# Experts of a mixture, two at a time in plain float32 in the two halves of the array's columns

## The chip, the cores and the metric

The program runs on one core of one Trainium2 chip, as one launch. The metric is device microseconds of the whole program, from its first to its last instruction and what the launch adds around them. Times of single instructions come from one profiled execution on that core, in microseconds from the start of its span.

## What is computed

Two transformer blocks run one after the other on 256 tokens of width 1024, all in float32. The first block (two layers: attention with a gated MLP, a pooling mixer, and after each a product-key expert layer) and the mixer of the second block are not touched by the change. The change is in the last layer, a hierarchical mixture of experts, which every token enters with two of 32 experts:

```python
def hier_moe(v, w_grp, b_grp, w_exp, b_exp, w_gate, w_up, w_down):
    ...
    w = p_grp * p_in / jnp.sum(p_in, axis=-1, keepdims=True)
    expert_id = g_sel * MOE_EXPERTS_PER_GROUP + e_sel
    combine = jnp.einsum('tk,tke->te', w, jax.nn.one_hot(expert_id, MOE_N_EXPERTS, dtype=f32))
    y = jnp.zeros(vt.shape, f32)
    for e in range(MOE_N_EXPERTS):
        hdn = jax.nn.silu(vt @ w_gate[e]) * (vt @ w_up[e])
        y = y + (combine[:, e:e + 1].astype(hdn.dtype) * hdn) @ w_down[e]
    return y.reshape(bsz, seq, d).astype(v.dtype)
```

Per expert w_gate and w_up are 1024 x 512 and w_down is 512 x 1024. All 32 experts' weights are read once: 192 units of 128 x 2048 floats (1 MiB each), six per expert: two for the gate, two for up, two for down.

## The kernel before

The last layer is `moe` (line 1405). It first makes the mixer's last product (`wout2`), the norm and the routing; `rk` then holds each token's place among its expert's tokens, up to CAP = 64 places per expert (a branch at the end, line 1710, serves experts with more; the trace shows none of it). The loop over the 32 experts follows (the `for n in range(32)` in `moe`). For one expert it does this:

- **Weights.** Each 1 MiB unit is loaded by SP's queue (`raw`, L161) into one of seven buffers (three of `raw_p`, four named `more`, carved from a large tile that the profile calls `room`). `halves` and `split` (L149, L150) then turn each half unit into a high part, by ScalarE, and the rest as a low part, by VectorE. Both are float32r, the type that TensorE takes in one pass. Five pairs of buffers hold the parts.
- **Tokens.** `place` and `gather` (L1542, L1550, L1553) make, for four experts at once, one-hot matrices and with them the gathered tokens `xg`, high and low parts side by side as 2 x 64 columns.
- **Gate and up.** `hidden` calls `lin2` (L1595, L1596): stationary are the 128 columns of an expert's tokens (64 high, 64 low), moving the weights' high part and then the low part, 512 columns each. That is 32 products for gate and up.
- **Merge and transpose.** The high and the low rows are added and turned by products with `pair` (L1618), Silu and the product of gate and up follow (L1621, L1622), and a split of the result into `hT`.
- **Down.** 16 more products in `lin2`, then the places' rows times their weights: `y` (L1634, L1635, or L1639 for one half of the columns, kept in plain float32).
- **Scatter.** Products with the one-hot `GT` add `y` to four accumulators in PSUM (L1645). `back` (L1582 to L1584) makes `GT` and the weights of the places.

The order on each engine is set when the program is built: the calls above are recorded, the small ones (`jobs`) placed by a rate between the products of `lin2`, and a scheduler then moves instructions where dependences allow. Each engine, and SP's queue of loads, then runs its list in order; a load waits until its buffer's last reader is done.

Of the kernel before, what the change touches and what calls it, by code (L numbers as in the profile page):

```python
# [9 lines left out]
F32 = mybir.dt.float32  # L10
F32R = mybir.dt.float32r
# [19 lines left out]
class Carve:  # L31
    """tiles of one stage, all float32 or integer, in [lo, hi) KB of larger tiles"""
# [37 lines left out]
def weave(main, other, rate):  # L70
    """main with rate steps of other after each of its own"""
    owed = 0.0
    for _ in main:
        owed += rate
        while owed >= 1:
            next(other, None)
            owed -= 1


def both(a, b):  # L80
    """steps of a and b in turn"""
# [11 lines left out]
def early(it, n):  # L93
    """the same, but n items ahead are made"""
    q = []
    for v in it:
        q.append(v)
        if len(q) > n:
            yield q.pop(0)
    yield from q  # L100


class Net:
    def __init__(self, es, tc, A):
# [5 lines left out]
        self.hl_p = ep(tc.tile_pool(name="hl_p", bufs=3))  # L110
        self.rings()
        self.nhl, self.more_hl = 0, []
# [20 lines left out]
    def room(self, es, *kbs):  # L133
        """large float32 tiles"""
# [18 lines left out]
    def rings(self, more=(), first=()):  # L153
        """where the loads go in turn: first, and then more and the three of raw_p over and over"""
# [9 lines left out]
    def halves(self, ap):  # L164
        r = self.raw(ap)
        w = ap.shape[-1] // 2
        for j in range(2):
            k = self.nhl % (3 + len(self.more_hl))
            self.nhl += 1
            hi, lo = self.more_hl[k - 3] if k > 2 else (self.hl_p.tile([P, 1024], F32R, tag=t, name=self.nm(t))  # L170
                                                        for t in ("hi", "lo"))
# [12 lines left out]
    def lin_steps(self, units, N, K, targets):  # L184
        """targets: (psum [128, N], fn(k) -> (hi, lo) stationary [128, 128]); a step for every k"""
# [13 lines left out]
    def squares(self, x, tt, h, parts):  # L199
        """parts[:, 2 * tt + h] = sum of squares of half a row, over the row's 1024"""  # L200
# [3 lines left out]
    def rstd(self, x=None, parts=None):  # L204
        """[128, 2] of (mean square of x's rows + eps) ** -0.5"""
# [29 lines left out]
    def trans_split(self, src, hh, hl, nk, scale=None, bias=None, full=None):  # L235
        """src [128, 2, nk*128] -> hh, hl [128, nk, 256], optionally scaled and shifted per row of the result"""
# [28 lines left out]
    def bcast(self, dst, cols):  # L265
        """dst [128, 1024]: every row holds the 1024 values of cols [128, 8]"""
# [20 lines left out]
    def mod_pair(self, l, order, pool, works):  # L287
        """chunks of 512 values, for the sequence and for the context; works run in between"""
# [24 lines left out]
    def mod_rows(self, l, n0, n1, pool):  # L313
        """chunks for the sequence alone, by the tensor engine; a step for every half unit"""
# [21 lines left out]
    def mod_chunks(self, l, n0, n1, cb):  # L336
        """the same by the vector engine, cb: the condition in every row; a step for every unit"""
# [13 lines left out]
    def mod_scale(self, g_cols, sc_cols):  # L351
        """g * (1 + sc) as [128, 8]"""
# [4 lines left out]
    def resid(self, x, accs, gb, pool, then=None):  # L357
        """x += gb * accs;  accs[tt][half] psum"""
# [10 lines left out]
    def resid_rstd(self, x, accs, gb, pool):  # L369
        """the same, and the new rows' inverse root mean squares"""  # L370
# [5 lines left out]
    def mixer0(self, x, pool):  # L376
# [53 lines left out]
        # keys twice, for the two halves of the partitions  # L430
# [5 lines left out]
        def axial(dst, src, tt, nh):  # L436
            """dst [128, nh, 64] = rope(src)"""
# [16 lines left out]
        # [(head of the pair, d), pair, t]  # L454
# [25 lines left out]
        # attention, a pair of heads at a time  # L480
# [53 lines left out]
        # gMLP  # L534
# [51 lines left out]
    def peer_pre(self, l, x, r, hh, hl, pool):  # L586
        """the modulated second norm, transposed and split; r: the inverse root mean squares of x"""
# [6 lines left out]
    def peer(self, l, after):  # L594
        """-> accs[tt][half], psum tiles of the [256, 1024] result"""
# [7 lines left out]
        def rows(i, n):  # L603
            """S[:, i:i + n], within one half"""
# [7 lines left out]
        # the routing's working space lies where the last products come  # L612
# [11 lines left out]
        # of the sums of two sorted sixteens the best sixteen have (a + 1) * (b + 1) <= 16:  # L624
        # rows of 16, 8, 4 and 2 columns hold them, in the order of a * 16 + b
# [35 lines left out]
        def routing():  # L661
# [10 lines left out]
            for tt in range(2):  # L672
# [14 lines left out]
                # column c of the candidates: row a and column b  # L687
# [1293 lines left out]
```

## Time and profile before

| | |
|---|---|
| time, median of 3 runs | 2728.44 us (2725.46 to 2731.94) |
| span of the profiled execution | 2725.8 us |
| TensorE busy over the span | 2633.1 us (97%) |
| VectorE busy | 2128.4 us (78%) |
| ScalarE busy | 1728.3 us (63%) |
| read from memory | 592.49 MB, 219 GB/s over the span |

The profile gives the span of the execution (first to last instruction) and no other time of its own; the median of the runs is 2.6 us above it. In the last quarter of the span, from about 2106 us on, lies the layer that is changed: of forty equal slices of the span, the last nine show transfers at some 340 GB/s, TensorE busy at 90% or more and both other engines at 80 to 90%, until the last slice.

### The profile page before, as it was taken

What the parts mean: (1) busy time and instruction counts of PE and PEld (TensorE: products, weight loads), DVE (VectorE), ACT (ScalarE), POOL (GpSimd) and SP (SyncE); (2) the same over time, 40 slices, a digit from 0 to 9 for tenths busy, and PEclk for the clock granted to TensorE, in tenths of its full rate; (3) what the DMA queues carried; (4) which work ended last, traced back from release to release, by engine and by line L of the source; (5) the groups of instructions that cost most, each with busy time, mean ns of one, the idle gap of its engine ahead of it and who ended that gap; (6) DMA issues with size and microseconds to landing.
All of it is one profiled execution on the core that took longest, in us unless ns stands there. A gap on an engine that the chain in (4) does not pass through costs nothing. (4 is left out here: it accounts for less than half of the span.)

```text
span 2725.8 us, 42575 instructions
## 1 busy us (share of the span) xinstructions
PE 2633.1 (97%) x16114; PEld 2250.3 (83%) x16114; DVE 2128.4 (78%) x3881; ACT 1728.3 (63%) x3024; POOL 24.8 (1%) x28
## 2 busy tenths in 40 slices
PE   8989999999999999999999999998999899999997
PEld 4679999999888879999999888886777777677775
DVE  3666998897589864998898656667767898888887
ACT  4454547886444544454887544455665798888886
POOL 0000000000000000000000000000000000000000
PEclk9999999999999999999999999999999899999999
DMA  6454554335589833455333655554426799899994
GB/s 262 185 187 170 195 188 176 127 139 197 219 337 365 336 119 141 171 195 193 140 140 140 223 186 185 196 184 146 156 93 217 272 363 340 339 340 348 338 347 186
DMA packets 86818, 598.47 MB, mean 220 GB/s; under 512 B 10430, under 2 KB 12366, under 8 KB 15694
## 3 DMA queue, kind: packets, MB, share of 16 engines
q1 hardware_dynamic: 80608, 583.73, 58.0%
q10 hardware_dynamic: 5998, 11.94, 1.3%
q8 instruction: 129, 2.11, 0.3%
q14 instruction: 83, 0.68, 0.1%
HBM read 592.49 MB, written 3.15 MB: 219 GB/s over the span
## 5 line engine op out<-in xcount | busy, mean ns | idle before, releaser
L150 DVE TENSOR_TENSOR lo<-raw,hi 128x1024 fp32r<-128x1024 f32 x744 | 897.4, 1218 | 283.6 <-ACT hi L149 281.7
L149 ACT CAST hi<-raw 128x1024 fp32r<-128x1024 f32 x744 | 770.6, 1050 | 428.2 <-PE mm L740 247.4
L739 PE MATMUL mm<-hh,hi 128*128 128x256 f32 x2048 | 577.4, 282 | 0.0
L741 PE MATMUL mm<-hh,lo 128*128 128x256 f32 x2048 | 568.3, 278 | 0.3 <-DVE lo L150 0.3
L740 PE MATMUL mm<-hl,hi 128*128 128x256 f32 x2048 | 567.8, 277 | 0.0
L177 PE MATMUL acc<-hi,hh 128*128 128x512 f32 (+1 forms) x1312 | 512.4, 394 | 2.1 <-ACT hh L149 1.6
L179 PE MATMUL acc<-hi,hl 128*128 128x512 f32 (+1 forms) x1312 | 514.2, 392 | 0.0
L178 PE MATMUL acc<-lo,hh 128*128 128x512 f32 (+1 forms) x1312 | 513.5, 391 | 0.1
L740 PEld LDWEIGHTS mm<-hl,hi 128*128 128x128 f32 x2048 | 386.2, 189 | 0.0
L741 PEld LDWEIGHTS mm<-hh,lo 128*128 128x128 f32 x2048 | 384.9, 188 | 0.8 <-DVE lo L150 0.5
L739 PEld LDWEIGHTS mm<-hh,hi 128*128 128x128 f32 x2048 | 385.0, 188 | 0.0
L150 DVE TENSOR_TENSOR lo<-room,hi 128x1024 fp32r<-128x1024 f32 x270 | 319.6, 1220 | 49.3 <-ACT hi L149 48.2
L149 ACT CAST hh<-room 128x256 fp32r<-128x256 f32 x272 | 109.3, 406 | 316.8 <-PE acc L178 306.8
L177 PEld LDWEIGHTS acc<-hi,hh 128*128 128x128 f32 x1312 | 247.0, 188 | 56.4 <-issue 2.2
L178 PEld LDWEIGHTS acc<-lo,hh 128*128 128x128 f32 x1312 | 247.4, 189 | 52.0 <-DVE lo L150 0.9
L179 PEld LDWEIGHTS acc<-hi,hl 128*128 128x128 f32 x1312 | 247.2, 188 | 51.4
L149 ACT CAST hi<-room 128x1024 fp32r<-128x1024 f32 x270 | 273.0, 1057 | 14.6 <-PE acc L179 12.9
L1596 PE MATMUL mm<-lo,xg 128*128 128x512 f32 x512 | 230.8, 451 | 19.1 <-DVE lo L150 19.1
L1595 PE MATMUL mm<-hi,xg 128*128 128x512 f32 x512 | 202.3, 396 | 0.0
L150 DVE TENSOR_TENSOR hl<-room,hh 128x256 fp32r<-128x256 f32 x272 | 111.7, 422 | 92.5 <-ACT hh L149 92.2
L1596 PEld LDWEIGHTS mm<-lo,xg 128*128 128x128 f32 x512 | 96.2, 188 | 72.5 <-DVE lo L150 45.1
L791 PE MATMUL mm<-room 128*128 128x128 f32 x1024 | 132.3, 275 | 0.4 <-ACT room L785 0.4
(469 smaller groups left out, 3512.9 us busy)
## 6 DMA issues: line engine op xcount, KB each, us to landing
raw<-in_dn SPq DMA_DIRECT2D x128, 1024.0 KB, 4.8
room<-in_moe SPq DMA_DIRECT2D x109, 1024.0 KB, 5.6
raw<-in_up SPq DMA_DIRECT2D x103, 1024.0 KB, 4.8
raw<-in_moe SPq DMA_DIRECT2D x83, 1024.0 KB, 5.4
room<-in_up SPq DMA_DIRECT2D x25, 1024.0 KB, 6.7
raw<-in_modt SPq DMA_DIRECT2D x24, 1024.0 KB, 6.1
raw<-in_w2in SPq DMA_DIRECT2D x18, 1024.0 KB, 4.8
raw<-in_wq SPq DMA_DIRECT2D x16, 1024.0 KB, 4.8
```

The source lines that it names most:

```text
L149: self.nc.scalar.copy(hi, src)
L150: self.last_lo = self.nc.vector.tensor_tensor(lo, src, hi.bitcast(F32), ALU.subtract).ins
L177: mm(ps, xh, wh, start=start, stop=False)
L178: mm(ps, xh, wl, start=False, stop=False)
L179: mm(ps, xl, wh, start=False, stop=stop)
L739: mm(o, wh, hh[:, k, :], start=(k == 0), stop=False)
L740: mm(o, wh, hl[:, k, :], start=False, stop=False)
L741: mm(o, wl, hh[:, k, :], start=False, stop=(k == KD - 1))
L791: mm(ps[:, j * P:(j + 1) * P], B[:, j, :], Am[:, j, :], start=True, stop=True)
L1595: mm(ps, get(k + j), hi[:, w], start=(k + j == 0), stop=False)
L1596: mm(ps, get(k + j), lo[:, w], start=False, stop=(k + j == K - 1))
```

## The change

Experts go through the loop in pairs, 16 turns instead of 32. The weights are no longer split: TensorE reads the loaded units as plain float32, in which each product is two passes (two instructions). The tokens of a pair are gathered as plain float32 too (high and low parts are summed in PSUM by the gather). One expert's 64 places are stationary in columns 0 to 63 of the array and write partitions 0 to 63 of a PSUM tile, the other's in columns 64 to 127 write partitions 64 to 127, and the two experts' products alternate. The merge with `pair` falls away; four transposes serve both experts. Both halves of `y` are split for the scatter now, and one scatter serves the pair. The pool of split buffers is closed after `wout2` (whose product becomes a function of its own, `mix_out`), and its room, with that of other finished stages, becomes load buffers: 15 in all (three of `raw_p`, ten of the new pool, two carved). The kernel's comments are removed as well.

```diff
@@ class Net, __init__ and halves
-        self.hl_p = ep(tc.tile_pool(name="hl_p", bufs=3))
+        self.hl_es = ExitStack()
+        self.hl_p = self.hl_es.enter_context(tc.tile_pool(name="hl_p", bufs=3, side="right"))
...
@@ moe
+        buf = [None] * 3 + [rpool.tile([P, 2048], F32, name=f"w{j}") for j in range(nring)]
+        buf += [pool.tile([P, 2048], F32, name=f"w{nring + j}") for j in range(2)]
+        nring = len(buf)
+
+        def load(j, ap):
+            t = buf[j % nring]
+            if t is None:
+                t = self.raw_p.tile([P, 2048], F32, tag="raw", name=self.nm("raw"))
+            nc.sync.dma_start(t, ap)
+            return t
+
+        order = [(2 * q + e, u) for q in range(16) for u in range(6) for e in range(2)]
+        W = early((load(j, A["moe"][e, u]) for j, (e, u) in enumerate(order)), nring - 2)
...
-        def lin2(ps, W, K, get):
-            for k in range(0, K, 2):
-                hi, lo = next(W)
-                for j in range(2):
-                    w = slice(j * 512, (j + 1) * 512)
-                    mm(ps, get(k + j), hi[:, w], start=(k + j == 0), stop=False)
-                    mm(ps, get(k + j), lo[:, w], start=False, stop=(k + j == K - 1))
...
         def hidden(xs, W):
...
             out = []
             for j in range(2):
                 ps = self.mm()
-                lin2(ps, W, KD, lambda k: xs[:, k].rearrange("p a s -> p (a s)"))
-                t = pool.tile([P, 512], F32, tag=f"gu{j}", bufs=2, name=self.nm("gu"))
-                nc.scalar.copy(t, ps)
-                out.append(t)
-            return out
...
+                for u in range(2):
+                    Ws = [next(W) for _ in range(2)]
+                    for k in range(4 * u, 4 * u + 4):
+                        for e in range(2):
+                            mm(ps[e * CAP:(e + 1) * CAP, :], xs[:, k, e, :], Ws[e][:, (k % 4) * 512:(k % 4 + 1) * 512],
+                               start=(k == 0), stop=(k == KD - 1))
+                out.append(ps)
+            g = pool.tile([P, 512], F32, tag="g", bufs=2, name=self.nm("g"))
+            nc.scalar.activation(g, out[0], AF.Silu)
+            nc.vector.tensor_tensor(g, g, out[1], ALU.mult)
+            return g
+
+        def hid_T(g):
             ps = self.mm()
-            for j, t in enumerate(gu):
-                for f in range(4):
-                    mm(ps[:, (j * 4 + f) * CAP:(j * 4 + f + 1) * CAP], t[:, f * P:(f + 1) * P], pair,
-                       start=True, stop=True)
...
+            for f in range(4):
+                nc.tensor.transpose(ps[:, f * P:(f + 1) * P], g[:, f * P:(f + 1) * P], self.ident)
+            t = pool.tile([P, 4, 2, CAP], F32, tag="hT", bufs=2, name=self.nm("hT"))
+            nc.vector.tensor_copy(t.rearrange("p f a s -> p (f a s)"), ps)
             return t
 
         def down(hT, W, cw):
...
-                lin2(ps, W, 4, lambda k: hT[:, k].rearrange("p a s -> p (a s)"))
...
+                Ws = [next(W) for _ in range(2)]
+                for f in range(4):
+                    for e in range(2):
+                        mm(ps[e * CAP:(e + 1) * CAP, :], hT[:, f, e, :], Ws[e][:, f * 512:(f + 1) * 512],
+                           start=(f == 0), stop=(f == 3))
+                y = rpool.tile([P, 2, 512], F32R, tag="yr", bufs=3, name=self.nm("y"))
+                nc.scalar.activation(y[:, 0, :], ps, AF.Copy, scale=cw)
+                nc.vector.scalar_tensor_tensor(y[:, 1, :], ps, cw, y[:, 0, :].bitcast(F32), ALU.mult, ALU.subtract)
+                ys.append(y)
+            return ys
+
+        def scatter(a, GT, y, tt, start, stop):
+            for j in range(2):
+                mm(a, GT[:, tt * P:(tt + 1) * P], y[:, j, :], start=start and j == 0, stop=stop and j == 1)
...
+        for n in range(16):
+            q, o = n // 2, slice(2 * (n % 2), 2 * (n % 2) + 2)
+            g = hidden(Gs[q][1][:, :, o], W)
+            if prev is not None:
+                scatters(n - 1, *prev)
+            GT, cw = bk
+            if n % 2 == 0 and q < 7:
+                Gs[q + 1] = places(q + 1)
+            hT = hid_T(g)
...
+            prev = GT, down(hT, W, cw)
+        scatters(15, *prev)
...
@@ build
         net.hybrid(xn, pool, last, scaled)
+        pool = Carve((net.S2[0], 8, 64))
+        state = net.mix_out(x, pool)
         ws.close()
         upper.close()
-        pool = Carve((net.S2[0], 8, 64))
-        with tc.tile_pool(name="moe", bufs=1) as rpool:
-            net.moe(x, pool, rpool)
+        net.hl_es.close()
+        with tc.tile_pool(name="moe", bufs=1, reuse_waits="tile") as rpool:
+            net.moe(x, state, pool, rpool, 10)
```

Up to `wout2` the lists of all engines are the same as before (only two small loads of constants on ScalarE's queue stand elsewhere). From there two places matter.

TensorE in the middle of the loop, before: rows of `lin2` for one expert (L1595 and L1596 are the high and the low part of the weights), with the jobs among them.

```order
L1595 MATMUL mm_23974<-hi_23965,hT_23893 128x512
L1618 MATMUL mm_24019<-room_1438 128x64 x8
L1596 MATMUL mm_23974<-lo_23956,hT_23893 128x512
L1645 MATMUL acc_20345<-y_23996,GT_23721 128x512
L1550 MATMUL mm_24052<-G_23896,hh 128x256 x2
L1596 MATMUL mm_24033<-lo_20086,xg_23311 128x512
```

TensorE in the loop now: the end of one pair's up products (L1587), the transposes (L1598) and `back` (L1569, L1571), the down products (L1611) and the scatter (L1621) of their result. Buffers w_ and raw_ are loaded units, room_1438 is a carved unit or the tokens.

```order
L1587 MATMUL mm_20816<-w_20294,room_1438 64x512
L1587 MATMUL mm_20816<-room_1438 64x512
L1598 MATMUL mm_20847<-ident,room_1438 128x128 x4
L1569 MATMUL mm_20854<-ident,G_20706 128x128 x2
L1571 MATMUL mm_20854<-room_1438,G_20706 128x2 x2
L1611 MATMUL mm_20862<-room_1438 64x512
L1611 MATMUL mm_20862<-raw_20765,room_1438 64x512
L1611 MATMUL mm_20876<-raw_20767,room_1438 64x512
L1621 MATMUL acc_20351<-y_20873,GT_20755 128x512
L1621 MATMUL acc_20353<-y_20873,GT_20755 128x512
```

What moved: the products are 64 columns wide and alternate between two units, read as loaded; the small work stands between chains of them instead of between single products. A chain of L1587 or L1611 is broken by other work three times in a pair with an odd number and six times in one with an even number, where the gathers for the next four experts (L1551) stand in it too.

SP's queue of loads where the layer begins, before: `wout2`, and then the experts' units as split buffers come free.

```order
L161 DMA raw_20011<-in_wpg 128x2048
L161 DMA room_1438<-in_wout 128x2048
L161 DMA raw_20096<-in_wout 128x2048
L161 DMA room_1438<-in_moe 128x2048
L161 DMA raw_20130<-in_wout 128x2048
L161 DMA raw_20171<-in_wout 128x2048
L161 DMA raw_20422<-in_moe 128x2048
L161 DMA raw_20437<-in_moe 128x2048
L161 DMA raw_20454<-in_moe 128x2048
L161 DMA room_1438<-in_moe 128x2048 x2
```

The same place now:

```order
L161 DMA raw_20085<-in_wout 128x2048
L1462 DMA room_1438<-in_moe 128x2048 x2
L161 DMA raw_20119<-in_wout 128x2048
L161 DMA raw_20162<-in_wout 128x2048
L161 DMA raw_20196<-in_wout 128x2048
L1462 DMA raw_20408<-in_moe 128x2048
L1462 DMA raw_20410<-in_moe 128x2048
L1462 DMA raw_20412<-in_moe 128x2048
L1462 DMA w_20285<-in_moe 128x2048
L1462 DMA w_20286<-in_moe 128x2048
L1462 DMA w_20287<-in_moe 128x2048
```

What moved: the fourth unit of `wout2` goes through `raw_p` too, and behind the three `raw` units that follow it stand ten loads into new buffers (w_20285 to w_20294), which wait only for stages that end before `wout2` does or, the last of the ten, for one of its last products. Of the 192 loads these and the two carved ones make 15 that need no buffer of the loop to come free.

## Rows read from the trace of the kernel before

**Rows 1.** The page's first line.
```profile
span 2725.8 us, 42575 instructions
```
**Rows 2.** By stretch: length; busy PE, PEld, DVE, ACT, POOL; clock, DMA share, GB/s.
```profile
2106.60:2131.40 24.80, 13.60 (x93) 12.94 (x91) 18.08 (x54) 11.13 (x26) 6.55 (x4) 0.72 0.42 149
2131.40:2709.50 578.10, 556.97 (x2589) 414.92 (x2587) 511.92 (x535) 502.41 (x751) 0.00 (x0) 1.00 0.88 333
2709.50:2725.80 16.30, 1.99 (x5) 0.68 (x4) 5.99 (x12) 3.28 (x6) 1.38 (x2) 0.71 0.18 68
```
**Rows 3.** Groups of instructions in the loop: busy us, mean ns, idle before them.
```profile
L150 DVE TENSOR_TENSOR lo<-room,hi 128x1024 fp32r<-128x1024 f32 x216 | 254.1, 1219 | 30.6 <-ACT hi L149 30.0
L1596 PE MATMUL mm<-lo,xg 128*128 128x512 f32 x512 | 230.8, 451 | 19.1 <-DVE lo L150 19.1
L149 ACT CAST hi<-room 128x1024 fp32r<-128x1024 f32 x216 | 217.1, 1060 | 0.1
L1595 PE MATMUL mm<-hi,xg 128*128 128x512 f32 x512 | 202.3, 396 | 0.0
...
L1635 DVE SCALAR_TENSOR_TENSOR y<-mm,room,y 128x512 fp32r<-128x512 f32 x32 | 23.8, 744 | 1.0 <-ACT y L1634 1.0
...
L1634 ACT ACTIVATE y<-mm,room 128x512 fp32r<-128x512 f32 x32 | 22.2, 692 | 2.7 <-PE mm L1596 2.6
```
**Rows 4.** Waits in the loop: us in total, times, longest.
```profile
PEld mm L1596 <- DVE lo L150: 66.0, 125, 1.6
```
**Rows 5.** Timeline of TensorE, first stage: plain float32 products (start, us, count).
```profile
18.27 7.03 PE L297 MATMUL mm<-raw,silu_c 128*2 128x512 f32 x16 [3.34 <-DMA raw<-in_modw]
...
39.42 3.60 PE L297 MATMUL mm<-raw,silu_c 128*2 128x512 f32 x8
```
**Rows 6.** Timeline of TensorE: plain float32 products in halves of the array's rows.
```profile
77.60 1.12 PE L491 MATMUL mm<-kT,qT 64*128 64x512 f32 x2
...
79.52 1.42 PE L491 MATMUL mm<-kT,qT 64*128 64x512 f32 x4
80.86 0.60 PE L495 MATMUL mm<-lmask,ident 128*128 128x128 f32 x3
...
1942.96 1.16 PE L1282 MATMUL mm<-room 64*128 64x128 f32 x16
1944.05 0.50 PE L179 MATMUL acc<-hi,hl 128*128 128x512 f32 x1
```
**Rows 7.** Weight loads: one line's durations, and a stretch of the timeline.
```profile
L1104 PEld LDWEIGHTS mm<-hi,flatr x32: 133/134/137, 1901.5 to 1923.2; 128*64 128x64 f32 x32
...
2099.73 0.39 PE L177 MATMUL acc<-hi,hh 128*128 128x512 f32 x1
...
2099.97 0.39 PE L178 MATMUL acc<-lo,hh 128*128 128x512 f32 x1
2099.97 0.19 PEld L179 LDWEIGHTS acc<-hi,hl 128*128 128x128 f32 x1
```
**Rows 8.** By stretch, as rows 2: three stretches of much loading.
```profile
10.00:25.00 15.00, 11.66 (x28) 2.13 (x26) 1.07 (x3) 4.40 (x10) 1.11 (x2) 1.00 1.03 415
...
2150.00:2225.00 75.00, 74.46 (x367) 58.95 (x366) 71.60 (x76) 69.79 (x106) 0.00 (x0) 1.00 0.97 375
2225.00:2675.00 450.00, 431.27 (x1989) 317.76 (x1987) 394.42 (x413) 388.19 (x582) 0.00 (x0) 1.00 0.91 342
```
**Rows 9.** Timeline of SP's queue where the layer begins.
```profile
2081.81 9.96 SPq L161 DMA_DIRECT2D raw<-in_moe  x3
...
2100.88 0.33 SPq L161 DMA_DIRECT2D room<-in_moe  x1
```
**Rows 10.** Timeline: the last expert's last down product.
```profile
2709.11 0.40 PE L1596 MATMUL mm<-lo,hT 128*128 128x512 f32 x1
```
**Rows 11.** By stretch, as rows 2: TensorE's clock around the routing.
```profile
2115.00:2116.00 1.00, 0.00 (x0) 0.00 (x0) 0.90 (x5) 1.00 (x2) 0.53 (x1) 0.73 0.72 303
...
2129.00:2130.00 1.00, 1.00 (x10) 1.00 (x10) 0.00 (x0) 1.00 (x4) 0.00 (x0) 0.94 0.00 0
```

## What is predicted, and how

> **What bounds the kernel now.** I read the busy time by stretch first, since the change touches one stage: of the span of 2725.8 us [rows 1] the loop over the experts takes 2131.4 to 2709.5, 578.1 us, 36.1 us for two experts [rows 2]. In it TensorE is busy 557.0 us, VectorE 511.9 and ScalarE 502.4, and the loads move 333 GB/s at a DMA share of 0.88 [rows 2]. All are nearly full, so the next question is which one the others wait for. The groups of the loop show TensorE idle for 19.1 us before the products with the low parts, all of it put down to VectorE's split, and the list of waits shows that their weight loads waited 66.0 us for it, never over 1.6 us at a time [rows 3, 4]. So TensorE is the bound at 96%, and the splitting stands right behind it: 432 half units at 1219 ns on VectorE (of these the x216 row shows those loaded into `room`) [rows 3]. Removing the splits alone would give back some 21 us (578.1 less 557.0). What decides is the TensorE time of the new products and then the loads.
>
> **What leaves.** VectorE and ScalarE lose the splits, which are most of their work in the loop; what is left to them (a copy, a Silu, a product, two y of 692 and 744 ns each [rows 3]) is under 8 us in a pair of experts and stays off the path but for the waits counted below. TensorE loses 96 one-pass products a pair, at the 0.23 to 0.24 us that lie between starts of such products in a row [rows 7], about 22.3 us, and the merging products (L1618).
>
> **The price of a new product.** Plain float32 takes two passes. In the first stage eight passes more cost 7.03 - 3.60 = 3.43 us, 0.429 a pass of 512 columns, with 0.17 behind the last one [rows 5]. A pair has 48 such products, 96 passes, 41 us one after the other. So all hangs on whether the two experts' passes overlap. No row of before has two products side by side in halves of the columns. The nearest are two heads in halves of the rows, plain float32 too: two passes took 1.12 us, four passes of two heads 1.42 [rows 6]. One after the other the second head would have added 0.86, and it added 0.30. That is what in-order issue gives where the second head's first pass runs beside the first head's second: three slots, 3 x 0.429 + 0.17 = 1.46. A longer chain of 16 passes of 128 columns agrees: 1.16 us, against 16 x 0.107 + 0.17 = 1.88 serially and nine slots, 9 x 0.107 + 0.17 = 1.13, with overlap [rows 6]. So a chain of m alternating products takes m + 1 slots where halves overlap and 2m where they don't. From the long chain a slot is (1.16 - 0.17) / 9 = 0.110, 3% over a pass; I take 0.44 us for 512 columns. I take the overlap for the columns as well, since the rows' halves are the nearest case, and keep 2m slots as the other end.
>
> The Trainium skill (TensorEngine Tiling (Array Packing), Theoretical Speedup) gives up to 2x for a dimension of at most 64, columns as well as rows; the rows' halves agree in the row above, and for columns no run here shows it yet. By that page the pair needs the 52.5 slots below.
>
> **The sum for a pair on TensorE.**
> - Products: 48, in three chains in one pair and six in the next (the order shown with the change), so 48 + 4.5 slots: 52.5 x 0.44 = 23.1 us.
> - Change between halves and the whole array: after the four passes the next product began at 80.86, 0.05 after the third slot's end (79.52 + 1.29); after the long chain at 1944.05, 0.10 after its ninth slot [rows 6]. 0.10 at both ends of 4.5 chains: 0.9 us.
> - Other products: 16 gathers of half the 0.23, 8 scatters of 0.23 (one-pass) and ten small passes at about 0.12 (a quarter of 0.429 and some reloading, an estimate): 1.84 + 1.84 + 1.2 = 4.9 us.
> - Waits in order: the transposes wait for the last up product's end (0.17) and VectorE's product (0.69, as the y of [rows 3]), the down products for VectorE's copy, which `back` mostly covers; each of two scatters waits for y's high part behind one product and then for the low part's 744 ns: 0.9 + 0.1 + 2 x 0.5 = 2.0 us.
>
> Together 30.9 us, 494 us for 16 pairs, instead of 578.1. The lower end is 25.5 (no breaks, no waits: 48 x 0.429 + 4.9), the upper about 34.5, if every break costs a us.
>
> **Start and end.** The splits of the first units that now stand between the norm's and the routing's steps go; I take 2130 for the loop's start instead of 2131.4. Behind the last product lie 16.3 us now [rows 2, 10], y, scatter, norm and output; I add 0.5 for the second half's low part. End of the span by TensorE: 2130 + 494 + 16.8 = 2641.
>
> **The loads.** A unit is 1.049 MB. The order now allows 15 units before the loop frees a buffer. The third `raw` one of them waits for the split of the last `wout2` unit, which in before freed its buffer at 2100.88 [rows 9]; ten more follow at up to 2.8 us each, so they have landed at about 2133, when the first buffers of the loop come free. From there 177 loads are left. At 375 GB/s, as in the 75 us after 2150 (DMA share 0.97), a load takes 2.80 us; at 415 GB/s, as in the first stage, with the other engines nearly idle (share 1.03), 2.53 [rows 8]. I take 2.66, between them, since the splits' traffic is gone but TensorE reads more: 2133 + 471 + 4 (last eight products) + 16.8 = 2625. With 2.80 it is 2649, with 2.53 it is 2601. So loads and TensorE come out within 16 us of each other; 15 buffers let each run ahead of the other, and the later one, TensorE at 2641, sets the end. The loads at the start cost nothing: SP's new loads ahead of `wout2`'s second unit wait for stages that are over by then, and wout2's own last unit, issued when its first is split (in before the first buffer so freed at 2081.81 [rows 9]), is needed only for its last quarter, past 2100.
>
> With the 2.6 us that lie between the median and this span: **2644 us**, 3.1% faster.
>
> **Rivals.**
> *Column halves don't overlap.* Both experts' weights pass through the same rows of the array, unlike the heads above. Then a pair costs 96 x 0.44 + 0.9 + 4.9 + 2.0 = 50.0 us, 800 us in all, and the end is 2130 + 800 + 16.8 = 2947, the time 2949, 8% slower. It decides from 36.2 us a pair ((2709.5 - 2130) / 16), that is 64.5 slots instead of 52.5. For it: no row shows columns. Against it: both rows of [rows 6]. Chance 0.12.
>
> *Weight loads come out from under the products.* Each pass loads its weights; 64 columns took 133 ns or more [rows 7]. If none of it were hidden, 96 x 0.134 = 12.9 us come on top: 43.8 a pair, time 2850. Against it: today the load of L179 starts while L178's product runs in the same rows, and products of 0.213 us (half a plain pass) follow every 0.23 [rows 7]. Chance 0.04.
> The Trainium skill (TensorE: Matmul & The Clock Gate, Part 3: Packing small matmuls) says that weight loads overlap running products only where the row group differs, and column halves share theirs, which would be this rival. The trace disagrees, by the load of L179 at 2099.97.
>
> *The loads stay at the loop's rate.* From 2225 on they ran at 342 GB/s with a share of 0.91 [rows 8]. If this is what the memory gives and not what the buffers allowed, a load is 3.07 us and the end 2133 + 543 + 20.8 = 2697, time 2700, 1% faster. Against it: 375 and 415 in the same rows. Chance 0.04.
>
> *The clock.* Where TensorE waits for loads it could fall to the lower level, 1.2 GHz. It fell (mean 0.73) at 2115 to 2116, some 2 us into the 9 us in which routing left it idle, and was back up at 2129 [rows 11]; in the loop, with waits of up to 1.6 us, it stayed at 1.00 [rows 2, 4]. New waits for loads last at most 2.66 x 2 less four steps of 0.88, 1.8 us. Should it fall, TensorE has no waits left, and the clock rises again; 10% of the loop at half clock costs 50 us. I put it in the upper end of the forecast's range.
>
> **Chances.** Forecast 0.80, no overlap 0.12, weight loads 0.04, loads at 342 GB/s 0.04. The range runs from 2602 (loads at 415 GB/s) to 2702 (34.5 us a pair, 2130 + 552 + 16.8 + 2.6 = 2701, or loads at 342); it leaves out 0.16 for the two slow rivals and 0.04 of the forecast's own misses. Faster by over 0.2%, about what a measurement of this kernel can tell from no change, 0.83 (forecast and the third rival, less 0.01 for sums of several misses), within it 0.01, slower 0.16.
>
> **What the profile will show.** Right: pairs of L1587 in chains with about 0.44 us a product, no busy time in L149 and L150 after 2106, and a loop of about 495 us at 390 GB/s or so. Products at 0.88 us each mean no overlap. A DMA share near 1.0 with TensorE waiting for w_ and raw_ buffers means that the loads set the end; TensorE gaps at L1598 and L1621 over 2 us a pair mean that I undersized the waits. A clock below 1.00 in the loop means the last rival.

## The result, and the profile after

The changed kernel takes 2654.7 us (median of 4 runs, 2653.3 to 2655.8), the kernel before beside it 2728.7 us: a ratio of 0.9725, 95% interval 0.9711 to 0.9739. The forecast was 2644 us, faster; the time lies 10.7 us above it and inside its range. Two terms of the sum were off, by 30 and by 15 us, in opposite directions, so that it came out so near is in part luck.

The span of its profiled execution is 2653.5 us, where [rows 1] has 2725.8. By stretch, the answer to [rows 2] for the changed kernel: routing, loop, end, and the middle of the loop (columns as there: length; busy PE, PEld, DVE, ACT, POOL; clock, DMA share, GB/s).

```profile
2135.00:2160.10 25.10, 14.59 (x99) 14.12 (x97) 15.11 (x52) 8.22 (x15) 5.70 (x4) 0.66 0.99 411
2160.10:2638.90 478.80, 449.94 (x2039) 179.16 (x2038) 60.08 (x125) 48.64 (x77) 0.00 (x0) 1.00 0.94 388
2638.90:2653.50 14.60, 1.47 (x4) 0.60 (x4) 6.09 (x11) 3.28 (x6) 1.38 (x2) 0.64 0.19 74
2225.00:2600.00 375.00, 349.53 (x1564) 136.27 (x1561) 45.65 (x95) 36.53 (x58) 0.00 (x0) 1.00 1.00 413
```

The loop over the experts takes 478.8 us instead of 578.1, 99.3 us less. It starts at 2160.1 instead of 2131.4, 28.7 us later. That late start is the surprise of this case: the instructions ahead of it are the same.

Inside the loop the splits are gone, and VectorE and ScalarE are nearly idle (60 and 49 us of 479). TensorE's timeline over one turn (start, us, count; L1587 gate and up, L1611 down, L1598 transposes, L1569 and L1571 `back`, L1621 scatter):

```profile
2295.87 0.63 PE L1598 MATMUL mm<-ident,room 128*128 128x128 f32 x4 [0.94 <-DVE room L1592]
...
2307.69 1.52 PE L1621 MATMUL acc<-y,GT 128*128 128x512 f32 x4 [0.77 <-ACT y L1614]
2309.14 3.65 PE L1587 MATMUL mm<-raw,room 128*64 128x512 f32 x16
2312.62 0.59 PE L1587 MATMUL mm<-w,room 128*64 128x512 f32 x1
2312.63 0.59 PE L1587 MATMUL mm<-raw,room 128*64 128x512 f32 x1
2313.05 0.59 PE L1587 MATMUL mm<-w,room 128*64 128x512 f32 x1
2313.06 0.59 PE L1587 MATMUL mm<-raw,room 128*64 128x512 f32 x1
...
2323.94 0.66 PE L1598 MATMUL mm<-ident,room 128*128 128x128 f32 x4 [0.85 <-DVE room L1592]
...
2325.42 4.48 PE L1611 MATMUL mm<-w,room 128*64 128x512 f32 x18 [0.27 <-issue]
2329.91 1.52 PE L1621 MATMUL acc<-y,GT 128*128 128x512 f32 x4
...
2335.78 1.52 PE L1621 MATMUL acc<-y,GT 128*128 128x512 f32 x4 [0.77 <-ACT y L1614]
...
2350.40 0.51 PE L1551 MATMUL mm<-G,hh 128*128 128x256 f32 x2
...
2351.07 1.07 PE L1587 MATMUL mm<-w,room 128*64 128x512 f32 x2
...
2357.80 0.63 PE L1598 MATMUL mm<-ident,room 128*128 128x128 f32 x4 [0.94 <-DVE room L1592]
```

What to see there: the passes of the two experts (w and raw) start 0.01 us apart, and the next two follow after 0.43 us. So a step, one product of two passes for each expert, takes 0.857 us for both. A turn, from one L1598 to the next, without gathers takes 28.07 us (2295.87 to 2323.94), one with gathers 33.86 (to 2357.80). Where other work cuts a chain behind an odd number of products, one product runs alone: the 18 passes at 2325.42 are nine products and take five steps (4.49 us), and the two passes at 2351.07 are one product that takes a whole step.

What TensorE waited for in the loop (us in total, times, longest):

```profile
PE mm L1598 <- DVE room L1592: 12.5, 14, 0.9
PE acc L1621 <- ACT y L1614: 10.8, 14, 0.8
PE mm L1611 <- issue: 4.0, 15, 0.3
PE mm L1611 <- DVE room L1600: 0.8, 1, 0.8
```

No load is in the list, though the loads run at a DMA share of 1.00 in the middle of the loop.

### The profile page after: what moved, and what is told of

The parts are those of the page before. It is cut to its first block, busy times and chain, and to the rows that moved or that the text cites. A ratio compares the mean times of both kernels' runs of the same rounds, so it can differ in the third digit from the quotient of the medians.

```text
span 2653.5 us, 39872 instructions
## 1 busy us (share of the span) xinstructions
PE 2556.4 (96%) x15570; PEld 2053.0 (77%) x15570; DVE 1672.7 (63%) x3465; ACT 1267.6 (48%) x2335; POOL 24.6 (1%) x28
## 5 line engine op out<-in xcount | busy, mean ns | idle before, releaser
L150 DVE TENSOR_TENSOR lo<-raw,hi 128x1024 fp32r<-128x1024 f32 x580 | 705.9, 1219 | 286.3 <-ACT hi L149 282.9
L149 ACT CAST hi<-raw 128x1024 fp32r<-128x1024 f32 x580 | 604.0, 1044 | 463.4 <-PE mm L737 289.4
L736 PE MATMUL mm<-hh,hi 128*128 128x256 f32 x2048 | 589.2, 288 | 0.0
L738 PE MATMUL mm<-hh,lo 128*128 128x256 f32 x2048 | 580.4, 283 | 0.0
L737 PE MATMUL mm<-hl,hi 128*128 128x256 f32 x2048 | 580.1, 283 | 0.0
L1587 PE MATMUL mm<-w,room 128*64 128x512 f32 x688 | 181.9, 595 | 0.0
L1592 DVE TENSOR_TENSOR room<-room,mm 128x512 f32<-128x512 f32 x16 | 11.0, 688 | 267.2 <-PE mm L1587 267.2
L1614 ACT ACTIVATE y<-mm,room 128x512 fp32r<-128x512 f32 x32 | 22.0, 687 | 248.8 <-PE mm L1611 248.8
L1587 PEld LDWEIGHTS mm<-w,room 128*64 128x64 f32 x688 | 56.1, 137 | 91.9 <-issue 89.4
L788 PEld LDWEIGHTS mm<-room 128*128 128x128 f32 x1024 | 123.9, 192 | 0.5 <-ACT room L782 0.5
## 6 DMA issues: line engine op xcount, KB each, us to landing
raw<-in_moe SPq DMA_DIRECT2D x39, 1024.0 KB, 10.4
room<-in_moe SPq DMA_DIRECT2D x24, 1024.0 KB, 10.7
```

The costliest lines, as they stand in the source:

```text
L149: self.nc.scalar.copy(hi, src)
L150: self.last_lo = self.nc.vector.tensor_tensor(lo, src, hi.bitcast(F32), ALU.subtract).ins
L736: mm(o, wh, hh[:, k, :], start=(k == 0), stop=False)
L737: mm(o, wh, hl[:, k, :], start=False, stop=False)
L738: mm(o, wl, hh[:, k, :], start=False, stop=(k == KD - 1))
L788: mm(ps[:, j * P:(j + 1) * P], B[:, j, :], Am[:, j, :], start=True, stop=True)
```

## Experiments

Every experiment shows its edit against the changed kernel unless it says otherwise.

### Where the 28.7 us ahead of the loop went

In the mixer ahead of the layer the delay is already there: the row at 1942.96 in [rows 6] stands 28.7 us later now. Further back, the one-pass products of 256 columns in the two product-key expert layers follow each other every 0.120 us instead of 0.113. First the kernel before, then the changed one:

```profile
339.83 0.28 PE L739 MATMUL mm<-hh,hi 128*128 128x256 f32 x1
339.94 0.28 PE L740 MATMUL mm<-hl,hi 128*128 128x256 f32 x1
340.05 0.28 PE L741 MATMUL mm<-hh,lo 128*128 128x256 f32 x1
```

```profile
339.75 0.28 PE L736 MATMUL mm<-hh,hi 128*128 128x256 f32 x1
339.87 0.28 PE L737 MATMUL mm<-hl,hi 128*128 128x256 f32 x1
339.99 0.28 PE L738 MATMUL mm<-hh,lo 128*128 128x256 f32 x1
...
1971.64 1.16 PE L1279 MATMUL mm<-room 64*128 64x128 f32 x16
```

What differs is where the tiles lie. The change puts the pool of hi and lo at the other end of the on-chip memory so that it can be closed, and hh and hl move with it. The theory: the place of the operands sets the rate. The rival: something else in the program, or the run.

**e1**, the kernel before with this line alone:

```
-        self.hl_p = ep(tc.tile_pool(name="hl_p", bufs=3))
+        self.hl_p = ep(tc.tile_pool(name="hl_p", bufs=3, side="right"))
```

> The kernel before with one edit: the pool of split buffers hl_p is placed at the other end of the on-chip memory, so hi and lo, and with them hh, hl and everything above, get other addresses, the same as in the changed kernel. No instruction changes. Theory (placement): the changed kernel reaches its loop 29 us late (2160.5 against 2131.4) because one-pass products of 256 columns (L739 to L741) then follow each other every 0.120 us instead of 0.113; this kernel loses the same: 6144 products x 0.0067 = 41 us at most, less a few us that 512-column products gain (0.2267 against 0.229), so about 2728 + 29 = 2757 us (2750 to 2770), loop start near 2160. Rival (something else in the changed kernel, or the run, made the early stages slow): 2728 us, 0.113 us a product, loop start 2131.

Measured: 2754.5 us, ratio 1.0099 (1.0082 to 1.0115), 26 us slower than the kernel before.

**e2**, the changed kernel with the line undone, at the price of three load buffers:

```
-        self.hl_p = self.hl_es.enter_context(tc.tile_pool(name="hl_p", bufs=3, side="right"))
+        self.hl_p = ep(tc.tile_pool(name="hl_p", bufs=3))
...
-            net.moe(x, state, pool, rpool, 10)
+            net.moe(x, state, pool, rpool, 7)
```

> The changed kernel with the pool of split buffers back where it was before, and therefore never closed; 12 load buffers (seven new ones) instead of 15. Placement theory: products of 256 columns every 0.113 us again, loop start near 2131, and since the loop is bound by TensorE at some 30 us for two experts, 12 buffers do: 2655 - 29 = 2626 us (2620 to 2634). Rival (the 29 us have another cause): 2655 us. Rival (the loop needs the 15 buffers): loop start 2131 but loop longer than 479 us, with TensorE waiting for w and raw, time between 2630 and 2660.

Measured: 2625.9 us, ratio 0.9623 (0.9607 to 0.9639), 29 us better than the changed kernel. The loop takes the same 480 us with 12 buffers (2133.0 to 2613.1). Both runs say placement; the line that made room for buffers cost more than the buffers gave.

**e6, e7, e8** ask what about the placement. They take e2 and change only the order in which three pools are allocated, which shifts start addresses by 192 bytes or swaps neighbours:

```
 e6:  small, hl_p, hhl_p     (e2: hl_p, small, hhl_p)
 e7:  hhl_p, hl_p, small
 e8:  hhl_p, small, hl_p
```

> The kernel of e2_after_left with the small pool allocated ahead of hl_p: hi and lo move by 192 bytes, hh and hl stay. Start addresses modulo 256, from the built program: hi and lo 224, hh and hl 224 (before: 32 and 224; changed kernel: 224 and 224, but at the other end). If it matters that the loaded weights (hi, lo) start at 224: products of 256 columns every 0.120 us, 2626 + 29 = 2655. If it matters that both operands start alike: the same. If only the far end of the memory matters: 0.113 us and 2626.

> The kernel of e2_after_left with the pool of hh and hl ahead of hl_p and of small: hi and lo 32, hh and hl 32 modulo 256. If the start of hi and lo alone matters: 0.113 us, 2626. If it matters that both operands start alike: 0.120 us, 2655. If only the far end matters: 2626.

> The kernel of e2_after_left with hh and hl first, then small, then hl_p: hi and lo 224, hh and hl 32 modulo 256. If the start of hi and lo alone matters: 0.120 us, 2655. If it matters that both operands start alike: 0.113 us, 2626. If only the far end matters: 2626.

Measured: 2658.0, 2654.5 and 2662.5 us; all three lose what e2 had won (28.6 to 36.6 us). The stretch from 300 to 400 us in the first expert layer, for the changed kernel, e1, e2, e6, e7 and e8, counts TensorE's products at a full engine (the first x):

```profile
300.00:400.00 100.00, 100.00 (x836) 100.00 (x835) 91.34 (x258) 47.49 (x55) 0.00 (x0) 1.00 0.52 182
```

```profile
300.00:400.00 100.00, 100.00 (x836) 100.00 (x835) 91.52 (x268) 48.41 (x56) 0.00 (x0) 1.00 0.48 180
```

```profile
300.00:400.00 100.00, 100.00 (x883) 99.89 (x882) 96.29 (x287) 50.33 (x58) 0.00 (x0) 1.00 0.54 191
```

```profile
300.00:400.00 100.00, 100.00 (x836) 100.00 (x835) 91.54 (x263) 47.74 (x55) 0.00 (x0) 1.00 0.50 179
```

```profile
300.00:400.00 100.00, 100.00 (x836) 100.00 (x835) 91.52 (x258) 47.67 (x56) 0.00 (x0) 1.00 0.52 185
```

```profile
300.00:400.00 100.00, 100.00 (x851) 100.00 (x850) 92.84 (x269) 48.24 (x56) 0.00 (x0) 1.00 0.53 189
```

The four kernels in which hi and lo start at the same address modulo 256 as hh and hl (224 and 224, or 32 and 32) have 836, at either end of the memory. With 32 against 224 it is 883 in e2 and 877 in the kernel before, with 224 against 32 it is 851. So the far end and the start of hi and lo alone are out, and what counts is how the two operands of a product stand to each other. Only the starts 32 and 224 were tried: that the period is 256 bytes, and why the place counts, is not shown. The third expectation fell in part: e8 has unlike starts and gained little here, and it lost in the products of 512 columns, where the loaded operand is hh or hl and the moving one hi or lo (436 in the 100 us from 1620 against 448 in e6 and 444 in e2).

**e10** adds to e2 three load buffers, by drawing each hi and lo pair from one tile of 2048 columns and using these tiles as load buffers later (15 in all), with the starts of before (the lines that put these tiles among the buffers are left out here):

```
-            hi, lo = (self.hl_p.tile([P, 1024], F32R, tag=t, name=self.nm(t)) for t in ("hi", "lo"))
+            hl = self.hl_p.tile([P, 2048], F32R, tag="hl", name=self.nm("hl"))
+            hi, lo = hl[:, :1024], hl[:, 1024:]
```

> The changed kernel with the placement of before and 15 load buffers (three of them the split buffers), its order unchanged. TensorE bound theory: as with 12 buffers, about 31.0 us a pair, 2626 us (2621 to 2630). Rival (the three buffers more help): 2615 us or less.

Measured: 2633.5 us, above the range expected. The loop took 474.6 us instead of 480.1, but it started at 2143.0, ten us later than in e2: the rate fell early in the first expert layer, with nothing in the order to tell why. **e11** and **e12** ran e10 and e2 once more:

> The kernel of e10_place15 once more, unchanged. In its first profile TensorE's instructions in stretches of 25 us of the first expert layer fell from 223 (250 to 275 us) to 214 (325 to 350 us), while in the second layer most stretches had 223, and its time was 7 us above the sum. If the program fixes this (its addresses, its order), the same stretches show the same counts again. If it is a matter of the single execution, the stretches with 214 and those with 223 lie elsewhere.

> The kernel of e2_after_left once more, unchanged; its first profile had 223 TensorE instructions in most stretches of 25 us. If the program fixes the rate, 223 again in the same stretches. If it is a matter of the single execution, some stretches fall to 214 to 218, and the time is up to 10 us longer than 2626.

Measured: 2634.3 and 2625.0 us; e12 had 883 in the stretch above once more. From the profile of e11:

```profile
250.00:275.00 25.00, 25.00 (x223) 1.00 0.39 133
300.00:400.00 100.00, 100.00 (x852) 1.00 0.53 189
325.00:350.00 25.00, 25.00 (x214) 1.00 0.52 186
1200.00:1300.00 100.00, 100.00 (x851) 1.00 0.52 188
```

The first layer began as in e10 (223, 214, and 852 in the 100 us), but the second had 851 where e10 had 863. The kernel e9 below has TensorE's and VectorE's instructions of e10 up to the loop, at the same addresses, and had 877 in the first of these two stretches of 100 us. So with the better starts TensorE can run at either rate, and what tips it within one execution stays open. With equal starts it stayed at the lower rate in the stretches above, in all four kernels.

### What the columns' halves give

**e5** leaves the loads and the number of products as they are, and puts 20 of the 24 steps of a turn in one half, so that its output is no longer the mixture's (the gate and up chains are shown, the flags and the down chains, changed alike, left out):

```
-            mm(ps[e * CAP:(e + 1) * CAP, :], xs[:, k, e, :], ...
+            d = e if k == 0 else 0
+            mm(ps[d * CAP:(d + 1) * CAP, :], xs[:, k, e, :], ...
```

> The changed kernel, order and loads untouched, but from the second step of each chain on the second expert's products go to the first expert's half of the columns (and are added into its rows, so the output is not the mixture's): of 24 steps a pair 20 have both products in one half. Theory (a step of two products costs the time of one only because they run in different halves): those 20 steps cost 1.71 us instead of 0.86, 17.1 us a pair, 274 us in all, and the time is about 2929 us (2900 to 2945). Rival (products of 64 columns are cheap wherever they stand, and alternating helps only through weights or buffers): within 30 us of 2655.

Measured: 2861.2 us, 206 more. The rows (two passes, one product each, alternating between the experts):

```profile
2382.48 1.02 PE L1588 MATMUL mm<-raw,room 128*64 128x512 f32 x2
2383.34 1.02 PE L1588 MATMUL mm<-w,room 128*64 128x512 f32 x2
2384.20 1.02 PE L1588 MATMUL mm<-raw,room 128*64 128x512 f32 x2
```

A product now takes 0.86 us by itself, twice its share of a step. The time lies below the range expected: a turn without gathers took 41.27 us, 13.2 more and not 17.1, since the order did not stay as I expected it. The scheduler put all eight scatters of a turn between the up chain and the transposes, where they fill the wait for VectorE and cut no step.

**e3** ran all products of one expert ahead of the other's, each in its own half (the down chains are shown, gate and up changed alike):

```
-                for f in range(4):
-                    for e in range(2):
+                for e in range(2):
+                    for f in range(4):
```

> The changed kernel with the two experts' products one after the other (all of a chain of the one, then all of the other) instead of alternating; same products, same loads, same halves of the columns. Theory (alternating products of the two column halves run side by side, a product of two passes costing 0.43 us instead of 0.86): 24 steps a pair that now run singly cost 48 x 0.857 = 41.1 us instead of 20.6, some 20.5 us a pair more, 329 us in all: 2984 us (2950 to 3000), loop near 808 us. Rival (the halves of the columns do not matter, the products are just cheaper than thought): 2655 us.

Measured: 2857.4 us, between the two. It is no clean control, and its output is not the mixture's, for a cause that stays open. From its timeline, at the joint between the last down chain (L1610) and the next gate chain (L1586), which uses the other half:

```profile
2413.45 1.08 PE L1610 MATMUL mm<-w,room 128*64 128x512 f32 x3
2413.95 0.64 PE L1586 MATMUL mm<-w,room 128*64 128x512 f32 x1
2414.37 0.59 PE L1610 MATMUL mm<-w,room 128*64 128x512 f32 x1
2414.43 0.59 PE L1586 MATMUL mm<-w,room 128*64 128x512 f32 x1
2414.80 0.59 PE L1610 MATMUL mm<-w,room 128*64 128x512 f32 x1
```

TensorE starts the next chain in the free half while passes of the former are still to come, so even chains written one behind the other overlap at their ends. Besides, this order asks for one expert's units first: a single wait of TensorE for a load reached 9.0 us, and the mean clock from 2200 to 2800 was 0.95. Of its time only this much is used here.

**e4** leaves out the second expert's products but for the first of each chain (a turn has four chains, so four remain; the expectation says three). Gate and up are shown, the down chains changed alike:

```
-                        for e in range(2):
+                        for e in range(2 if k == 0 else 1):
```

> The changed kernel without all but the first product of each chain for the second expert of a pair (42 of 48 ... that is, of 48 products a pair 24 of the first and 3 of the second expert remain); loads, gathers, transposes, scatters stay. The output lacks these parts. Theory (full overlap: the second expert's products ride along free): a step of the first expert alone still takes two passes, 0.857 us, so the time stays within 5 us of 2655. Rival (the halves share part of the path, as reading the moving data, and a step of two costs more than a step of one): below 2640, by 16 x 24 x the difference per step.

Measured: 2626.6 us, 28 less. The number is the rival's, but its reason is not met. The step did cost the same without its second product (eight passes, four products of one expert, next work 3.58 us later):

```profile
2396.87 3.65 PE L1587 MATMUL mm<-w,room 128*64 128x512 f32 x8
2400.45 0.50 PE L1551 MATMUL mm<-G,hh 128*128 128x256 f32 x2
```

Four steps of two products take the same 3.65 us at 2309.14 above. What shrank lay between the chains: a turn took 26.7 us without and 30.5 with gathers. No step could be cut in two any more, and in turns with gathers the last of these (2400.45 to 2401.50) now stood where the changed kernel waits 0.94 us for the transposes; how much each gave was not separated. That made the cut steps and the waits the next suspects.

### What is left in the loop

**e9** uses the placement and the buffers of e10, and ties every product of the loop behind the one ahead of it, in an order that changes work only between whole chains:

```
             g = hidden(Gs[q][1][:, :, o], W)
             if prev is not None:
-                scatters(n - 1, *prev)
+                scatters(n - 1, *prev, 1)
+            if more:
+                gathers(q + 1, range(2))
             GT, cw = bk
-            if n % 2 == 0 and q < 7:
-                Gs[q + 1] = places(q + 1)
             hT = hid_T(g)
...
+            if more:
+                gathers(q + 1, range(2, 4))
             prev = GT, down(hT, W, cw)
-        scatters(15, *prev)
+            scatters(n, *prev, 0)
+        scatters(15, *prev, 1)
```

> The placement of before (hi and lo at 32, hh and hl at 224 modulo 256; the split buffers are reused as three load buffers, 15 in all) and a fixed order of TensorE in the loop: the two products of a step always side by side, scatters, gathers, transposes and back only between whole chains, so that they also fill the waits for VectorE. TensorE's sum for a pair: 24 steps x 0.857 = 20.6, scatters 1.9, transposes and back 1.2, breaks 0.4, hT 0.3: 24.4 us, 28.4 with gathers, about 416 us in all. Theory (TensorE at 31.0 us a pair set the end so far, the loads stand right behind it at 12 x 2.5 = 29.9 us a pair): now the loads bind, 177 loads after 2133 at 2.497 us = 2575, with the last products and the tail 2595 of span, time 2598 us (2590 to 2607), TensorE waiting for loads, DMA share 1.0. Rival (loads do not bind yet): 2131 + 416 + 15 + 3 = 2565 us. Rival (breaks and split steps cost nothing that matters): 2626 us.

Measured: 2614.8 us (2606.5 to 2617.5), ratio 0.9577 (0.9559 to 0.9595), the fastest kernel here. Its loop takes 452.6 us (2136.4 to 2589.0), 22.0 less than that of e10, which has the same buffers and placement and the order of the changed kernel: so much the cut steps and the waits had cost, as far as the loads let it show. In the profile, TensorE's waits, and a stretch of 50 us:

```profile
PE mm L1570 <- DMA w<-in_moe: 11.0, 10, 1.3
...
PE mm L1570 <- DMA hl<-in_moe: 5.5, 6, 1.3
```

```profile
2130.00:2140.00 10.00, 10.00 (x56) 7.67 (x57) 1.23 (x5) 3.63 (x5) 0.00 (x0) 0.77 0.01 2
...
2350.00:2400.00 50.00, 44.61 (x211) 19.92 (x210) 4.62 (x10) 4.91 (x8) 0.00 (x0) 1.00 1.01 421
```

Now TensorE waits for loads and for little else, at 421 GB/s, while early turns run at 26.2 to 26.4 us (the expectation's mean is 26.4) and late ones, two together, at 59.7, which is 24 loads at 2.49. The miss against 2598 has two parts. The profiled execution took 2606.5 us, and its part is the start: all buffers were full and the loads idle from 2130 to 2140, since the first one is freed only some us into the loop, which began at 2136. The three other executions took 2613.3 to 2617.5, and where they lost the rest is not shown.

## Why the prediction was right, and where it was not

- **The bound and what leaves.** Right: TensorE was the bound and stays it in the changed kernel; the splits' work went away without a trace on the path.
- **The price of a product.** Right that the halves overlap; the lag between them was wrong and the slot with it mis-sized. I took m + 1 slots of 0.44 us for m products, read from halves of the rows [rows 6], where the second half seemed to lag by one pass, as in-order issue would have it. In halves of the columns the two start 0.01 us apart, a chain of m takes m slots of 0.428, and the extra slot appears only where a chain is cut behind an odd product. 20.6 us of whole steps a turn instead of the 23.1 taken; e5 shows the other end, 0.86 us a product.
- **Other products, breaks and waits.** Undersized by about as much, 10.4 us a turn instead of 7.8. Gathers cost 5.8 us a turn that has them (33.86 less 28.07), of which 32 products at 0.12 are 3.84 and the cuts the rest; a turn waits 0.85 for the transposes, 0.27 for hT and 0.77 for one y, and each of two scatters takes 1.45 us where its four products need 0.92. The two misses cancelled, which is luck: the mean of a turn with gathers and one without is 30.97 us, the prediction had 30.9.
- **Sixteen turns.** Failed by 15.2 us: 494 predicted, 478.8 measured. The steady turn was multiplied by 16. But the first period, from the first L1598 (2177.89) to the second, takes only 24.1 us: there all eight scatters stand between the up chain and the transposes, where they cut no step and fill the wait for VectorE.

```profile
2200.07 2.11 PE L1621 MATMUL acc<-y,GT 128*128 128x512 f32 x8
2202.02 0.60 PE L1598 MATMUL mm<-ident,room 128*128 128x128 f32 x4
```

  The second period takes 31.9. Only seven of the eight sets of gathers lie in the loop, so that the last three periods are 28.1 us each, and the loop's two ends, ahead of the first L1598 and behind the last, make 28.8 together.
- **The start.** Failed by 30.1 us: 2130 taken, 2160.1 measured. The step was that lists which are the same up to `wout2` take the same time. The edit to the pool's side stood in the diff, and I costed its instructions, not its addresses. e1, e2 and e6 to e8 show that the addresses cost it.
- **The end.** 14.6 us instead of 16.8; why was not followed up.
- **The sum.** 2640.8 + 30.1 - 15.2 - 2.2 = 2653.5, the span. Two figures of the prediction are wrong beside it, and no term rests on them: the loop of before splits 379 half units (216 from `room` and 163 from `raw`), not 432, and the range's lower end lacks the 2.6 us between span and time (2604 instead of 2602).
- **The loads.** Right that they come out near TensorE and do not bind; undersized in rate. 394 GB/s was taken between two rows of [rows 8], 421 came (e9), 2.49 us a load. The Trainium skill (Perfetto Trace Analysis, Roofline) bounds a single active core by its 16 DMA engines, at about 435 GB/s; the 421 at a share of 1.01 agree with such a bound.
- **The rivals.** No overlap of column halves: out, by the rows at 2312.62 and by e5. The Trainium skill's factor of two (TensorEngine Tiling (Array Packing), Theoretical Speedup) is met in full, 0.86 us against 0.43; a factor of two makes 48 slots a turn, and the 52.5 that the prediction gives beside that page hold its own lag of a pass as well. Exposed weight loads: out. The groups of weight loads in the loop show

```profile
L1587 PEld LDWEIGHTS mm<-w,room 128*64 128x64 f32 x688 | 56.1, 137 | 91.9 <-issue 89.4 <-DMA w<-in_moe 0.8 <-DMA raw<-in_moe 0.3
```

  that is, 137 ns each under passes that follow every 0.428 us, no slower than the 0.429 of [rows 5], whose weights are two columns. So the rule that a weight load overlaps only where the row group differs (the Trainium skill, TensorE: Matmul & The Clock Gate, Part 3) does not hold for these halves. Loads at 342 GB/s: out. The clock: 1.00 over the whole loop.

## What to carry to other kernels

Two halves of the array's columns run plain float32 products at twice the rate of one, but only while the partner of each product is next to it: count the steps that other work cuts in two, and put it between whole chains. When a diff moves a pool, read the start addresses of the operands of every hot product, not only of those that the change is about, since equal instruction lists are not equal times. And multiply a steady turn only by the turns that are steady.

## What the hardware showed that was not expected

- Products of 256 columns with both operands starting alike modulo 256 bytes came every 0.120 us, with the starts of before every 0.113 for most of the time (836 against 877 to 883 in 100 us, though e10 and e11 had 852 there). That is 26 to 32 us of the whole program (e1 against the kernel before, e6 against e2). The Trainium skill (TensorE: Matmul & The Clock Gate, Part 2: What happens when you issue a matmul) says that weights are loaded through a read port of their own and take nothing from the running product; here the place of the loaded operand relative to the moving one changed the rate, so the measurement decides; what the two share is not shown.
- For products of 512 columns with the roles swapped the effect was smaller and had another sign: 448 in 100 us with equal starts (e6), 444 with those of before (e2), 436 with the starts of e8.
- The two halves of the columns do not keep one order between them. A product's two passes stand one behind the other (`raw` twice, then `w` twice in the rows of e5), yet in the changed kernel the first passes of both experts start 0.01 us apart and the second ones 0.43 later. At the joint shown under e3, passes of the next chain stand between passes of the former one in the other half.
